# Stick-breaking attention summed by parts, with the value projection moved into half-size products

## The chip, the cores and the metric

The kernel runs on one core of a Trainium2 chip. The metric is the device time of one execution in microseconds (us), lower is better. Before the change three runs gave a median of 1948.08 us, from 1947.18 to 1949.51. The execution that was profiled took 1945.62 us.

## What is computed

One layer of a sequence model on a sequence of 1024 tokens with 1024 channels, all in float32. The part that the change touches is the mixer: a modulated RMS norm gives `h`, one projection of `h` gives q, k, v, three convolution inputs and two gates, and a stick-breaking attention with 16 heads of 64 channels runs on q, k, v:

```python
z = jnp.einsum('bhqd,bhkd->bhqk', qb, kp) * inv_sqrt          # strictly causal: s < t
log_not = jnp.where(mask, jax.nn.log_sigmoid(-z), 0.0)
excl = lax.cumsum(log_not, axis=3, reverse=True) - log_not
log_a = jax.nn.log_sigmoid(z) + excl
a = jnp.where(mask, jnp.exp(log_a), 0.0)
outs.append(jnp.einsum('bhqk,bhkd->bhqd', a, vp))
```

So the weight of key s for query t is sigmoid(z_ts) times the product of (1 - sigmoid(z_tj)) over the keys j between s and t. Then come a short gated convolution as a second branch, a projection of each branch, a merge by gates, an output projection, and a gated feed-forward network, each with a residual add.

## The kernel before, in words

**Number format.** Every matmul operand is split into a rounded part `hi` and a remainder `lo`, and a product is three matmuls: hi*hi, hi*lo, lo*hi. A split costs a ScalarE copy (`hi`) and a VectorE subtraction (`lo`).

**Half-size products.** Sections of the combined projection, and the feed-forward network, use a Strassen-Winograd scheme: a 1024x1024 product becomes seven products with 512 rows of weights and 512 tokens (`half_prod`, L117, twelve matmuls of 512 columns each). The weights' sums (`ws`, L587 to L590) are made on GpSimd. The factors of `h` are made once by `factors` (L342): it adds the two halves `hh` and `hl` of `h` back together (L348), makes the differences (L350 to L354), and splits the four results, which are called factor 5, 4, 6 and 3 (L356). Factors 5 and 4 stay in SBUF (`ft`); 6 and 3 go to DRAM (`d_t`) and are loaded back (L579, L581).

**Stages, in the order of time.**
1. Start, L142 to L330: modulation sums, the norm, and `h` made channel block by channel block (`make_h`, L260: two ScalarE passes and one GpSimd subtraction for each). TensorE already multiplies each finished block into the first seven of eight token blocks of the first 512 columns (`real`, L304). The order of the work here is pinned by `in_order`. The transposed input `xt` is kept in SBUF for this stage alone.
2. Projection by token blocks, the loop at L400: three chunks of 512 columns (the first half of v, then two halves of k), eight token blocks each, 24 matmuls of 512 columns for a block. A v block is split by `finish_v` (L391) and stored to `d_v`. A k block goes through `finish_k` (L369): square on ScalarE, sum on VectorE, reciprocal root on GpSimd (L113, L114), scaling on VectorE, four transposes on TensorE (L382), split, store to `d_k`. The steps of `factors` are spread over the k blocks.
3. Gates, the loop at L582: 20 sections of seven half-size products, first q (`put_q` after it), then the two convolution inputs (`put_u`), then the two gates. `later` drains the work that a section leaves over into the next products. Weight splits rotate through four buffers (`GS`), so ScalarE and VectorE run at most a few splits ahead of TensorE.
4. Attention: a generator `attention` (L756) emits 128 steps, one for a head h and a block i of 128 queries with n = 128(i+1) keys. `att_scores` (L691): two matmuls for each 512 keys into `z`; ScalarE takes a sigmoid of -z into `pt` (L705) and a sigmoid of z into `sg` (L706); VectorE runs a reversed running product over `pt` (the scan, L710) and multiplies `sg` by it, one place shifted (L712). One step later `att_trans` (L715) transposes `sg` on TensorE (L726) and splits it (L729, L730); for every second block, three steps later, `att_av` (L734) multiplies it by v (L741, L742), adds the two halves (L745, L746) and stores the head's rows of `d_ya` with a DMA on the SyncE queue (L748).
   Between these steps `fill` inserts pieces of `fillers` (L789) in proportion to the attention work done so far (`FILL`, `ATT`, `TAIL`): first the second half of v (L790 to L812, 384 matmuls of 256 columns), then the third convolution input (L814) and the second branch's projection (L840), 768 matmuls of 512 columns. `HEAD` pieces are put ahead of the first scores while the first head's q, k and v are loaded (L870 to L873).
5. The first branch's projection (L908 on), the output projection, the feed-forward network and its down projection.

A scheduler orders the instructions of each engine at build time; each engine then runs its own list strictly in that order and waits on semaphores. The DMAs that SyncE and ScalarE issue stand in those engines' lists too.

Of the kernel before, what the change touches and what calls it, by code (L numbers as in the profile page):

```python
# [8 lines left out]
F32 = mybir.dt.float32  # L9
# [7 lines left out]
P = 128  # L17
# [12 lines left out]
def block_kernel(tc, x, x_t, cols, ada_1, ada_2, ada_row, w_q, w_kv, w_v1, w_cg, w_a, w_b, w_o, w_g, w_u, w_d, out):  # L30
# [47 lines left out]
    d_t = {q: drp.tile([P, 2, 4, 512], F32, name=f"d_t{q}") for q in (6, 3)}  # L78
# [62 lines left out]
    sw = open_w("wpa", 3, 6)  # L141
# [17 lines left out]
    xt = sp.tile([P, KT, T], F32, name="xt")  # L159
# [13 lines left out]
    def load_wq(qt):  # L173
        wp, nraw, bufs = wps
        raw = wp.tile([P, 1024], F32, tag="raw", bufs=nraw, name=nm("raw"))
        nc.sync.dma_start(raw, w_kv[0, qt])
# [159 lines left out]
    ftx = ExitStack()  # L336
    ftp = ftx.enter_context(tc.tile_pool(name="phft", bufs=1, side="right", reuse_waits="tile"))
    ft = {q: ftp.tile([P, 2, 4, 512], F32R, name=f"ft{q}") for q in (5, 4)}
# [52 lines left out]
    def finish_v(ps, i, ch):  # L391
        vs = ap.tile([P, 8, P], F32R, tag="vs", bufs=3, name=nm("vs"))
        pv = ps.rearrange("p (h d) -> p h d", d=DH)
        nc.scalar.activation(vs[:, :, :DH], pv, AF.Copy)
        nc.vector.tensor_tensor(out=vs[:, :, DH:], in0=pv, in1=vs[:, :, :DH].bitcast(F32), op=ALU.subtract)
        nc.scalar.dma_start(d_v[8 * ch:8 * ch + 8, :, i, :].rearrange("h p d -> p h d"), vs.bitcast(F32))

    GR, NG, GS = 2, 2, 4
    tails = []
    for cc in range(3):  # L400
        w = wq if cc == 0 else [load_w(w_kv[cc, j]) for j in range(4)]
        for i in ((5, 6, 0, 1, 2, 3, 4, 7) if cc == 0 else range(8)):
# [15 lines left out]
            if (cc, i) == (2, 4):  # L418
# [32 lines left out]
    def w_of(sec, m):  # L451
        return w_q[m] if sec == 5 else w_cg[sec, m]
# [213 lines left out]
    for pt in pts:  # L666
        nc.gpsimd.memset(pt[:, D:D + 1], 0.0)
# [682 lines left out]
```

## Time and profile before

| | |
|---|---|
| median of 3 runs | 1948.08 us |
| the profiled execution, its own time | 1945.62 us |
| its span, first to last instruction | 1943.8 us |
| mean granted TensorE clock | 0.986 of full speed |
| TensorE busy (with matmul latency) | 1853.6 us, 95% |
| VectorE / ScalarE / GpSimd busy | 1462.3 / 864.6 / 673.7 us |
| stages by TensorE's own first and last instructions: start and token blocks to | about 204.6 us |
| gates to | 621.4 us |
| attention to | 1093.6 us |

How to read it: a matmul's row shows its latency, not what it costs when matmuls follow each other. A 512-column matmul shows some 0.39 us, but starts of neighbours stand 0.23 us apart. So TensorE's pace is read from how many matmuls fall into a stretch in which it never waits. "A <-B" behind a row names the engine and line whose end the instruction waited for.

### The profile page before, as it was taken

Reading aid. Unit: us, or ns where it says so; the run is one execution under the profiler, and the core shown is the slowest. Engines: PE = TensorE matmul, PEld = TensorE weight load, DVE = VectorE, ACT = ScalarE, POOL = GpSimd, SP = SyncE. Lnnn points to the kernel's source line nnn. Section 1 sums busy time; section 2 is a strip of 40 time slices with the busy share of each in tenths; the row PEclk is TensorE's granted clock in tenths of the full one; section 3 lists DMA queues with packets and bytes.
Section 4 is the critical chain, followed back from the end, with each engine's and each line's share of the span. In section 5 each row is a group of like instructions: output and inputs, shape, how many; then the busy total and the mean of one; then the engine's idle time right before and its main releaser. Section 6 shows DMA issues by size and latency. Waiting matters only on the chain.

```text
span 1943.8 us, 25154 instructions
## 1 busy us (share of the span) xinstructions
PE 1853.6 (95%) x8869; PEld 1519.5 (78%) x8869; DVE 1462.3 (75%) x1927; ACT 864.6 (44%) x1597; POOL 673.7 (35%) x475
## 2 busy tenths in 40 slices
PE   7899999998999999998999999979999999999899
PEld 4678767777888888887888788867888888878587
DVE  8865687778664799998999644499988788743854
ACT  4442343223333677776777421464444434422221
POOL 3694547978231001111000000065454444301713
PEclk8899999999999999999999999999999999999999
DMA  6465544334445756559554535323343334399566
GB/s 276 162 208 172 190 154 160 136 114 152 170 171 197 214 158 189 169 167 302 161 161 128 189 130 193 133 82 136 146 173 152 141 143 171 119 347 321 218 221 224
DMA packets 151149, 347.47 MB, mean 179 GB/s; under 512 B 15088, under 2 KB 52208, under 8 KB 149104
## 3 DMA queue, kind: packets, MB, share of 16 engines
q1 hardware_dynamic: 74000, 218.80, 34.4%
q10 hardware_dynamic: 76016, 123.40, 17.6%
q0 software_dynamic: 1008, 3.67, 0.5%
q8 instruction: 70, 1.15, 0.2%
q14 instruction: 55, 0.45, 0.1%
HBM read 235.19 MB, written 110.62 MB: 178 GB/s over the span
## 4 chain that ended last, share of the span: by engine, by line
PE 43%; DVE 10%; issue 3%; DMA 3%; ACT 2%; POOL 1%; ACTq 0%; SPq 0%; DVEq 0%; POOLq 0%
PE e L122 6%; PE e L124 6%; PE e L123 6%; PE e L1203 3%; PE e L1204 3%; PE e L1202 3%; PE pj L785 3%; PE pj L786 3%; PE pj L787 3%; DVE pt L710 2%; DVE wlo L965 2%; PE e L1020 1%; PE e L1022 1%; PE e L1021 1%; PE tr L726 1%
## 5 line engine op out<-in xcount | busy, mean ns | idle before, releaser
L710 DVE TENSOR_TENSOR_SCAN pt<-pt,dm 128x256 f32<-128x256 f32 (+7 forms) x128 | 173.9, 1363 | 5.3 <-ACT pt L705 5.1
L123 PE MATMUL e<-big,whi 128*128 128x512 f32 x352 | 138.0, 392 | 7.8 <-DVE big L127 7.8
L122 PE MATMUL e<-big,whi 128*128 128x512 f32 x352 | 137.7, 392 | 0.8 <-ACT c L1118 0.8
L124 PE MATMUL e<-big,wlo 128*128 128x512 f32 x352 | 137.5, 391 | 0.0
L1203 PE MATMUL e<-wlo,f 128*128 128x512 f32 (+1 forms) x319 | 123.1, 386 | 9.5 <-DVE wlo L965 9.5
L124 PE MATMUL pj<-big,wlo 128*128 128x512 f32 x320 | 127.0, 398 | 5.1 <-DVE wlo L127 5.1
L113 POOL TENSOR_SCALAR rs_m<-ss 128x1 f32<-128x1 f32 x8 | 2.0, 245 | 365.3 <-ACT xn L1035 365.3
L122 PE MATMUL pj<-big,whi 128*128 128x512 f32 x320 | 128.0, 400 | 0.4 <-ACT whi L438 0.4
L276 PE MATMUL pj<-whi,big 128*128 128x512 f32 x352 | 116.3, 410 | 11.6 <-ACT big L263 8.9
L123 PE MATMUL pj<-big,whi 128*128 128x512 f32 x320 | 127.1, 397 | 0.0
L705 ACT ACTIVATE pt<-z,rq 128x512 f32<-128x512 f32 (+2 forms) x192 | 112.3, 587 | 30.5 <-PE z L704 17.6
L1204 PE MATMUL e<-whi,f 128*128 128x512 f32 (+1 forms) x319 | 121.8, 382 | 0.0
L1202 PE MATMUL e<-whi,f 128*128 128x512 f32 (+1 forms) x319 | 118.5, 383 | 2.0 <-ACT fs L1142 1.4
L127 DVE TENSOR_TENSOR c<-e,c 128x512 f32<-128x512 f32 x154 | 102.8, 681 | 21.1 <-PE e L124 21.1
L829 POOL TENSOR_TENSOR ybl<-cy,ybh 128x512 fp32r<-128x512 f32 x16 | 29.0, 1810 | 255.7 <-ACT ybh L828 242.9
L438 ACT ACTIVATE whi<-raw 128x512 fp32r<-128x512 f32 x116 | 72.7, 633 | 94.4 <-PE pj L123 32.6
L706 ACT ACTIVATE sg<-z,rq 128x512 f32<-128x512 f32 (+1 forms) x192 | 112.7, 590 | 1.3 <-DVE mb L851 1.3
L127 DVE TENSOR_TENSOR c<-pj,c 128x512 f32<-128x512 f32 x140 | 93.2, 681 | 24.3 <-PE pj L124 24.1
L127 DVE TENSOR_TENSOR wlo<-ws,whi 128x512 fp32r<-128x512 f32 x80 | 73.6, 939 | 50.0 <-ACT whi L438 49.8
L730 DVE TENSOR_TENSOR atl<-tr,ath 128x512 fp32r<-128x512 f32 (+1 forms) x192 | 100.3, 544 | 10.7 <-ACT ath L729 10.3
L127 POOL TENSOR_TENSOR ws<-raw,raw 128x512 f32<-128x512 f32 x41 | 57.9, 1412 | 144.1 <-DMA raw<-w_cg 80.7
L729 ACT ACTIVATE ath<-tr 128x512 fp32r<-128x512 f32 (+1 forms) x192 | 90.4, 498 | 37.8 <-PE tr L726 12.7
(250 smaller groups left out, 5641.9 us busy)
## 6 DMA issues: line engine op xcount, KB each, us to landing
f<-d_f SPq DMA_DIRECT2D x77, 512.0 KB, 4.4
d_f<-fs ACTq DMA_DIRECT2D x70, 512.0 KB, 2.6
raw<-w_cg SPq DMA_DIRECT2D x40, 512.0 KB, 3.4
mada<-ada ACTq DMA_DIRECT2D x32, 512.0 KB, 4.2
raw<-w_g SPq DMA_DIRECT2D x24, 512.0 KB, 3.2
raw<-w_u SPq DMA_DIRECT2D x23, 512.0 KB, 3.2
d_k<-khl ACTq DMA_DIRECT2D x32, 256.0 KB, 2.2
d_q<-gt ACTq DMA_DIRECT2D x32, 256.0 KB, 2.1
```

Of the source, the lines that this page charges most:

```text
L122: nc.tensor.matmul(ps, wh[:, k, :], fh[:, k, :], start=(k == 0), stop=False)
L123: nc.tensor.matmul(ps, wh[:, k, :], fl[:, k, :], start=False, stop=False)
L124: nc.tensor.matmul(ps, wl[:, k, :], fh[:, k, :], start=False, stop=(k == 3))
L127: eng.tensor_tensor(out=out, in0=a, in1=b, op=op)
L276: nc.tensor.matmul(ps, a, b, start=(k == 0 and q == 0), stop=(k == KT - 1 and q == 2))
L705: nc.scalar.activation(pt[:, off + s0:off + s0 + m], z[:, :m], AF.Sigmoid, scale=rq[:, 1, i, h:h + 1])
L706: nc.scalar.activation(sg[:, s0:s0 + m], z[:, :m], AF.Sigmoid, scale=rq[:, 0, i, h:h + 1])
L710: nc.vector.tensor_tensor_scan(out=pt[:, rev], data0=pt[:, rev], data1=dm[:, rev], initial=0.0, op0=ALU.mult, op1=ALU.add)
L730: nc.vector.tensor_tensor(out=tl[:, :nb, c0:c0 + P], in0=src, in1=th[:, :nb, c0:c0 + P].bitcast(F32), op=ALU.subtract)
L1202: nc.tensor.matmul(o, sh, w[0][:, c], start=(j == 0), stop=False)
L1203: nc.tensor.matmul(o, sh, w[1][:, c], start=False, stop=False)
L1204: nc.tensor.matmul(o, sl, w[0][:, c], start=False, stop=(j == NJ - 1))
```

## The change

Four things are done together.

- **Attention summed by parts.** With R_s the running product over the keys from s on, the weight of key s is R_(s+1) - R_s. Moved onto the values this gives o_t = v_t + sum over s of R_s (v_(s-1) - v_s). So the scan's result `pt` is transposed itself; the second sigmoid (L706), the multiplication (L712) and the buffers `sg` go. The matrix that multiplies R is the difference of neighbouring values. The term v_t is written to `d_ya` ahead of time, and `att_av` adds onto it with an accumulating DMA, which is issued from GpSimd instead of SyncE.
- **Values by channel, in half-size products.** v becomes four more sections of the gates loop, at its head (24 sections instead of 20). A new `put_v` shifts, subtracts (GpSimd), stores v to `d_ya`, transposes the difference (TensorE), splits it through one buffer `vs` and stores it to `d_v`. The v chunk of the token blocks and the v fillers go, so the loop over token blocks has two chunks, both of k.
- **Factors in place.** `xt` is kept until the factors are made, and the differences are made in place in `xt`; the 16 additions of L348 go. Factor 4 joins 6 and 3 in DRAM (`d_t`) and is loaded back into the gates' pool. The pool of raw weights in the first stages has two buffers instead of three.
- **Planning numbers.** `FILL` goes from 2.5*16*5.2 to 2*16*5.2, and `HEAD` from 10 to 4 pieces.

```diff
     def factors():
         for j in range(4):
-            b = [[mp.tile([P, 512], F32, tag=f"tb{e}{n}", bufs=1, name=nm("tb")) for n in range(2)] for e in range(2)]
-            for e in range(2):
-                for n in range(2):
-                    tt(nc.gpsimd, b[e][n], hh[n][:, 4 * e + j, :].bitcast(F32), hl[n][:, 4 * e + j, :].bitcast(F32), ALU.add)
-                yield
+            b = [[xt[:, 4 * e + j, n * 512:(n + 1) * 512] for n in range(2)] for e in range(2)]
...
-    for cc in range(3):
-        w = wq if cc == 0 else [load_w(w_kv[cc, j]) for j in range(4)]
+    for cc in range(2):
+        w = wq if cc == 0 else [load_w(w_k[cc, j]) for j in range(4)]
...
-            if cc > 0:
-                tails.append(finish_k(ps, i, cc - 1))
-                next(tails[-1])
-            else:
-                finish_v(ps, i, 0)
-            for _ in range(2 if cc else 0):
+            tails.append(finish_k(ps, i, cc))
+            next(tails[-1])
+            for _ in range(2 if cc else 1):
                 next(ml, None)
...
-    gates = ([(5, j) for j in range(4)] + [(sec, j) for j in range(4) for sec in (1, 2)] +
+    gates = ([(sec, j) for sec in (6, 5) for j in range(4)] + [(sec, j) for j in range(4) for sec in (1, 2)] +
              [(sec, j) for sec in (4, 3) for j in range(4)])
...
+    def put_v(cf, m, n, left):
+        if n == 0:
+            nc.gpsimd.memset(cf[:, 1:2], 0.0)
+        else:
+            nc.gpsimd.tensor_copy(cf[:, 1:2], left[:, 513:514])
+        wt = g_tile()
+        tt(nc.gpsimd, wt, cf[:, 1:513], cf[:, 2:514], ALU.subtract)
+        nc.scalar.dma_start(d_ya[n][:, m, :], cf[:, 2:514])
+        yield
+        tr = ps_tr()
+        for i in range(4):
+            nc.tensor.transpose(tr[:, i * P:(i + 1) * P], wt[:, i * P:(i + 1) * P], ident)
+        vs = gp.tile([P, 2, 4, P], F32R, tag="vs", bufs=1, name=nm("vs"))
+        for h in range(2):
+            src = tr.rearrange("p (i d) -> p i d", d=P)[:, :, h * DH:(h + 1) * DH]
+            nc.scalar.activation(vs[:, h, :, :DH], src, AF.Copy)
+            tt(nc.vector, vs[:, h, :, DH:], src, vs[:, h, :, :DH].bitcast(F32), ALU.subtract)
+        nc.scalar.dma_start(d_v[2 * m:2 * m + 2, :, 4 * n:4 * n + 4, :].rearrange("h p i d -> p h i d"), vs.bitcast(F32))
...
         def later():
-            if pend:
+            if pendv:
+                next(pendv.pop(0), None)
+            elif pend:
                 put_q(*pend.pop(0))
-            elif g > 3:
+            elif g > 7:
...
             nc.scalar.activation(pt[:, off + s0:off + s0 + m], z[:, :m], AF.Sigmoid, scale=rq[:, 1, i, h:h + 1])
-            nc.scalar.activation(sg[:, s0:s0 + m], z[:, :m], AF.Sigmoid, scale=rq[:, 0, i, h:h + 1])
...
         nc.vector.tensor_tensor_scan(out=pt[:, rev], data0=pt[:, rev], data1=dm[:, rev], initial=0.0,
                                      op0=ALU.mult, op1=ALU.add)
-        nc.vector.tensor_tensor(out=sg[:, :n], in0=sg[:, :n], in1=pt[:, off + 1:D + 1], op=ALU.mult)
...
-                nc.tensor.transpose(tr[:, j * P:(j + 1) * P], sg[:, (b0 + j) * P:(b0 + j + 1) * P], ident)
+                nc.tensor.transpose(tr[:, j * P:(j + 1) * P], pt[:, off + (b0 + j) * P:off + (b0 + j + 1) * P], ident)
...
-        nc.sync.dma_start(d_ya[hf][e0:e0 + DH, pr, c0:c0 + 256], yv)
+        nc.gpsimd.dma_start(d_ya[hf][e0:e0 + DH, pr, c0:c0 + 256], yv, accum_op=ALU.add)
...
     def fillers():
-        for e in range(2):
-            w = []
...
-                nc.scalar.dma_start(d_v[8 + 4 * e:12 + 4 * e, :, i, :].rearrange("h p d -> p h d"), vs.bitcast(F32))
-                yield 1.3
         cb_w = {}
...
-    FILL = 2.5 * 16 * 5.2
+    FILL = 2 * 16 * 5.2
...
-    HEAD, TAIL = 10, 20.0
+    HEAD, TAIL = 4, 20.0
```

More of the change, by code (lines that the diff above doesn't have):

```diff
@@ L592, in block_kernel @@
             raws = two_raw(g + 1)
-        c11, c21, c12, c22 = (gp.tile([P, 512], F32, tag=f"c{q}", bufs=2, name=nm("c")) for q in range(4))
+        cfs = [gp.tile([P, 514], F32, tag=f"c{q}", bufs=2, name=nm("c")) for q in range(4)]
+        c11, c21, c12, c22 = (cf[:, 2:] for cf in cfs)
         def put(c, m, n):
-            if sec == 5:
+            if sec == 6:
+                if (m, n) == (j + 4, 1):
+                    return
+                f11, f21, f12, f22 = cfs
+                for a in (((f21, m, 0, None), (f22, m, 1, f21)) if m == j + 4 else ((f11, m, 0, None),) if n == 0 else
+                          ((f12, m, 1, f11),)):
+                    pv = put_v(*a)
+                    next(pv)
+                    pendv.append(pv)
+            elif sec == 5:
                 pend.append((c, m, n))
@@ L641, in block_kernel @@
                 pass
-        for _ in range((0 if sec == 5 else 3) if g + 1 < len(gates) else 50):
+        for _ in range((0 if sec >= 5 else 3) if g + 1 < len(gates) else 50):
             next(ml, None)
@@ L688, in block_kernel @@
     ats = {}
-    sgs = {}
+    ptof = {}
     def att_scores(h, i):
```

74 lines of the change are left out of this document (25 added, 49 removed).

## The prediction, made before the changed kernel was run

> **What bounds the kernel now.** I read the busy times by stage first, then the chain of waits, then each engine's costliest groups and TensorE's own waits inside the stages that change. Columns of the first view: stretch, then busy us (count) of TensorE, weight loads, VectorE, ScalarE, GpSimd, then clock and DMA.
>
> ```profile
> core 0: us, PE busy (x) PEld busy (x) DVE busy (x) ACT busy (x) POOL busy (x), PEclk, DMA share, GB/s
> 85.00:204.00 119.00, 116.91 (x543) 95.51 (x542) 67.72 (x84) 40.99 (x66) 84.09 (x69) 1.00 0.61 200
> 204.00:621.00 417.00, 402.51 (x1715) 316.26 (x1714) 305.37 (x365) 143.18 (x238) 240.18 (x156) 0.99 0.43 153
> 621.00:1094.00 473.00, 449.64 (x2757) 391.45 (x2756) 431.11 (x619) 341.60 (x732) 29.14 (x20) 0.99 0.63 186
> 1094.00:1184.00 90.00, 90.00 (x387) 72.29 (x386) 42.33 (x64) 19.44 (x32) 0.00 (x0) 1.00 0.42 142
> ```
> ```profile
> PE 43%; DVE 10%; issue 3%; DMA 3%; ACT 2%; POOL 1%; ACTq 0%; SPq 0%; DVEq 0%; POOLq 0%
> ```
>
> TensorE carries the chain in every stage. In the gates (204 to 621) VectorE has slack, in attention (621 to 1094) it is busy 431.1 of 473 us, so there TensorE and VectorE are both nearly full. Everything from 1094 on is untouched and I carry it over.
>
> TensorE's price per matmul: 90.00 us over 387 back-to-back matmuls of 512 columns is 0.2326 us. The next views give the token blocks' pace, a group of four transposes, and the value fillers.
>
> ```profile
> 111.13 0.39 PE L276 MATMUL pj<-whi,big 128*128 128x512 f32 x1
> ...
> 113.40 0.60 PE L382 MATMUL tr<-dm,qn 128*128 128x128 f32 x4
> 113.75 0.48 PE L276 MATMUL pj<-wlo,big 128*128 128x512 f32 x1
> 114.07 0.63 PE L276 MATMUL pj<-whi,big 128*128 128x512 f32 x2
> ```
> ```profile
> 621.50:632.50 11.00, 11.00 (x94) 10.99 (x93) 3.63 (x7) 2.97 (x7) 0.19 (x4) 1.00 1.01 285
> ```
>
> Ten matmuls start between 111.13 and 113.40: 0.227 us each. Four transposes take 0.35 us and slow the next matmul by 0.09: 0.0875 to 0.11 us each. A 256-column matmul takes 11.00/94 = 0.117 us.
>
> **The change part by part. TensorE's own work.** The value chunk of the token blocks goes: 8 x 24 = 192 matmuls x 0.227 = -43.6 us. The value fillers go: 384 x 0.117 = -44.9. Four gate sections come: 4 x 84 = 336 x 0.2326 = +78.2. Their 64 transposes: x 0.11 = +7.0. Net -3.3: the half-size products save little, because they bring transposes. So waits decide.
>
> **Waits before the gates.** The token blocks lose the value chunk, which needed no norm. Now the seven blocks begun in the start stage all end together and each needs the k norm:
>
> ```profile
> L371 ACT ACTIVATE qsq<-pj 128x512 f32<-128x512 f32 x16 | 9.5, 594 | 39.5 <-PE pj L276 28.7 <-DVE vs L395 3.4 <-DVE qn L376 2.6
> L373 DVE TENSOR_REDUCE qss<-qsq 128x8 f32<-128x512 f32 x16 | 10.9, 681 | 14.5 <-ACT qsq L371 14.5
> L376 DVE TENSOR_TENSOR qn<-pj,rs_r 128x512 f32<-128x512 f32 x16 | 11.0, 690 | 15.9 <-POOL rs_r L114 15.9
> ```
> ```profile
> L114 POOL TENSOR_TENSOR rs_r<-rs_m,nhalf 128x8 f32<-128x8 f32 x16 | 27.5, 1716 | 0.8
> L113 POOL TENSOR_SCALAR rs_m<-qss 128x8 f32<-128x8 f32 x16 | 4.3, 271 | 28.8 <-DVE qss L373 28.2
> ```
>
> In the changed program's TensorE list the transposes of three blocks stand in front of the second k chunk's first matmul. The third is ready after 0.6 + 0.7 + 3 x 2.0 (GpSimd, one at a time) + 0.7 = 8 us and some semaphore time, with about 1 us of matmuls to cover it. I take 8 us of idle TensorE (from 4, if the first blocks end earlier, to 14, if VectorE's factor splits push in between). All of the second chunk is queued behind. A long wait also costs clock:
>
> ```profile
> 206.86 0.57 PE L122 MATMUL pj<-ft,whi 128*128 128x512 f32 x1 [2.06 <-ACT whi L438]
> ...
> 208.94 0.63 PE L122 MATMUL pj<-ft,whi 128*128 128x512 f32 x1
> 209.36 0.63 PE L123 MATMUL pj<-ft,whi 128*128 128x512 f32 x1
> ...
> 210.62 0.39 PE L123 MATMUL pj<-ft,whi 128*128 128x512 f32 x1
> 210.84 0.39 PE L124 MATMUL pj<-ft,wlo 128*128 128x512 f32 x1
> ```
>
> Behind this 2.06 us wait eight matmuls start 0.43 us apart instead of 0.23: 1.6 us more. So +9.6 us. The wait quoted here, at the first gate, should go, since GpSimd has nothing ahead of the weight sums by then: -3.7 (at worst 0). *A rule beside it:* the Trainium skill, "TensorE: Matmul & The Clock Gate", section "What's actually happening", has the clock at half rate only after an idle window of about 3.4 us, for about 3.4 us. The length agrees with these rows, the threshold does not, as 2.06 us were enough; by the rule the last term would be -2.1 and the sum -8.8.
>
> The in-place differences move into the start stage's GpSimd list, between the subtractions that make `hl`; nine of them, 1.5 us each, fit in its idle time but may delay `hl`: +1 (0 to 5). The 16 additions that go (1.49 us each) stood beside matmuls: 0. Two raw buffers instead of three, and factor 4's trip through DRAM (2 MB more to load while the first two sections' 48 matmuls run): 0, up to 5 if that load is late.
>
> **The four value sections.** Per section TensorE needs 84 x 0.2326 + 16 x 0.11 = 21.3 us. Each has four `put_v`, and they share one buffer `vs`, so ScalarE's copy waits until the previous store has landed.
>
> ```profile
> L809 ACT ACTIVATE vs<-pj 128x256 fp32r<-128x256 f32 x16 | 6.3, 393 | 17.5 <-DMA d_v<-vs 11.4 <-PE pj L806 4.0 <-PE tr L726 2.0
> ```
> ```profile
> d_v<-vs ACTq DMA_DIRECT2D x8, 512.0 KB, 4.4
> d_t<-ts ACTq DMA_DIRECT2D x8, 512.0 KB, 3.4
> sqt<-d_q SPq DMA_DIRECT2D x32, 256.0 KB, 5.4
> d_f<-fs POOLq DMA_DIRECT2D x7, 512.0 KB, 7.4
> d_ya<-oy SPq DMA_DIRECT2D x64, 64.0 KB, 2.6
> ```
>
> The row shows that ScalarE already waits for such stores. A turn of the buffer is two copies (0.39 each), two VectorE halves (0.41 each, L810 below), 0.4 to issue, and the landing. The new store has 2 KB rows like `d_t<-ts` (3.4 us): 5.4 us a turn, 86 us for 16 turns against TensorE's 85. With the 4.4 us of `d_v<-vs` it is 6.4 x 16 = 102. While ScalarE waits, the weight splits behind it wait, and then TensorE. I take the landing near `d_t`: +5 (0 to 17).
>
> **Attention.**
>
> ```profile
> L710 DVE TENSOR_TENSOR_SCAN pt<-pt,dm 128x256 f32<-128x256 f32 (+7 forms) x128 | 173.9, 1363 | 5.3 <-ACT pt L705 5.1
> L730 DVE TENSOR_TENSOR atl<-tr,ath 128x512 fp32r<-128x512 f32 (+1 forms) x192 | 100.3, 544 | 10.7 <-ACT ath L729 10.3
> L712 DVE TENSOR_TENSOR sg<-sg,pt 128x128 f32<-128x128 f32 (+7 forms) x128 | 99.5, 783 | 5.7 <-ACT sg L706 0.6 <-DVE pt L710 0.5 <-ACT pt L705 0.5
> L810 DVE TENSOR_TENSOR vs<-pj,vs 128x256 fp32r<-128x256 f32 x16 | 6.6, 413 | 13.8 <-ACT vs L809 13.8
> ```
> ```profile
> L706 ACT ACTIVATE sg<-z,rq 128x512 f32<-128x512 f32 (+1 forms) x192 | 112.7, 590 | 1.3 <-DVE mb L851 1.3
> ```
> ```profile
> PE o L741 <- ACT ath L729: 8.9, 4, 4.4
> PE tr L726 <- DVE atl L730: 6.9, 13, 1.5
> ```
>
> VectorE loses L712 and L810, 106 us, and falls to about 325 busy; ScalarE loses 112.7 of 341.6. TensorE now: fillers 768 x 0.2326 = 178.6, values 44.9, scores 147,456 columns at 0.2326 per 512 = 67, L741/L742 512 x 0.117 + 128 narrow ones x 0.0875 = 71, transposes 576 x 0.0875 to 0.11 = 50 to 63; in all 412 to 425 of the 472 us from 621.4 to 1093.6. So 47 to 60 us are waits and stretched starts. With VectorE at 325 of some 405 us I let half of them go: -25 (0 to -50). What is late next is the scan itself, then ScalarE's `ath`.
>
> The start of attention gets worse: before, ten value pieces covered the load of head 0.
>
> ```profile
> 618.83 0.53 SPq L677 DMA_DIRECT2D sqt<-d_q  x1
> ...
> 627.63 0.54 SPq L680 DMA_DIRECT2D vt<-d_v  x1
> ```
>
> These loads spread over 9 us of SyncE's list and land 5.4 us later; four pieces of 6 matmuls cover 5.6 us. Three loads of weights stand ahead in the new list, the third waiting for a split. I take 4.4 us of wait and 1.6 of slow clock: +6 (0 to 11), all scores queued behind. `d_ya` moves from SyncE to GpSimd's list, where only 16 subtractions (29.1 us busy) stand; even landing in 7.4 instead of 2.6 us, the last store is not needed until some 10 us after attention's last product: 0, up to 5.
>
> **Sum.** -3.3 + 9.6 - 3.7 + 1 + 5 - 25 + 6 = -10.4 us. The profiled execution took 1945.6 us (span 1943.8), so 1935.2; it lies 2.5 under the median of 1948.1, which gives **1937.7 us**.
>
> **The rivals.**
> - *Attention is set free wholly.* All 50 us of stalls go and the first loads are covered: 25 + 6 less, 1906.7. For: VectorE at 91% explains most of it. Against: a TensorE in strict order never runs without waits.
> - *Slower: attention keeps its waits.* TensorE waits for a chain, sigmoid, scan, transpose, copy, and not for VectorE's load. The quoted waits end on `ath` (8.9) and `atl` (6.9), neither of which the change touches. Then the -25 is 0: 1962.7. It decides when fewer than 15 us go.
> - *The one buffer paces the value sections.* At a landing of 4.4 us +17 instead of +5: 1949.7; beyond that each further us costs 16.
> - *The change frees nothing because the DMA that adds is slow* and the first branch's projection waits: over 10 us a store; little speaks for it.
>
> **How the numbers follow.** Forecast (1923 to 1944) 0.45, wholly free 0.15, attention keeps its waits 0.22, the buffer 0.16, the last 0.02. A measurement tells about 0.2%, 4 us, from no change. Faster: 0.45 + 0.15, less a little for the forecast's edge, 0.58. The buffer's case lies half within 0.2%: same 0.12. Slower 0.30. The range runs from the wholly free case to the one that keeps its waits, 1906 to 1964.
>
> **What would show it.** Right: a TensorE wait of about 8 us on `qn` near 95 us; value sections of about 22.5 us each; gates ending near 670 instead of 621; attention about 408 long, VectorE near 325 in it; nothing changed behind. Wrong: an attention over 430 us whose transposes wait as before; `whi` splits waiting for `d_v<-vs` in every value section; TensorE waiting on `yr`.

## The result, and the profile after

The changed kernel takes 1956.89 us (median of 9 runs, 1951.95 to 1960.62); the kernel before, run beside it, 1947.18. The ratio is 1.006, with a 95% interval of 1.0043 to 1.0078: 0.6% **slower**, where 0.5% faster was forecast. The profiled execution took 1956.52 us, its span is 1954.7 (before: 1943.8), its granted clock 0.975 (0.986).

The first view is the stages: stretch, then busy us (count) of TensorE, weight loads, VectorE, ScalarE and GpSimd, then clock and DMA. First the start stage of the kernel before, then all stages of the changed one.

```profile
0.00:81.00 81.00, 59.83 (x214) 41.71 (x215) 70.48 (x121) 38.96 (x61) 34.66 (x31) 0.87 0.61 234
```
```profile
0.00:88.00 88.00, 65.95 (x213) 46.67 (x214) 76.45 (x121) 39.73 (x63) 45.42 (x39) 0.79 0.53 204
88.00:166.00 78.00, 66.24 (x304) 54.33 (x304) 50.27 (x65) 31.24 (x52) 46.42 (x41) 0.91 0.66 215
166.00:684.00 518.00, 501.75 (x2174) 397.91 (x2171) 360.68 (x460) 175.95 (x305) 293.97 (x210) 0.98 0.46 166
684.00:1105.00 421.00, 400.19 (x2367) 345.39 (x2368) 334.45 (x465) 248.12 (x515) 77.92 (x80) 0.98 0.71 195
1105.00:1195.00 90.00, 90.00 (x388) 72.36 (x387) 42.72 (x64) 20.42 (x33) 0.00 (x0) 1.00 0.39 135
```

```profile
L731 DVE TENSOR_TENSOR_SCAN pt<-pt,dm 128x256 f32<-128x256 f32 (+7 forms) x128 | 176.8, 1387 | 47.8 <-ACT pt L727 47.6
```

In attention VectorE fell from 431 to 334 us, as forecast, and it is no longer full: the row of the scan now has 47.8 us of idle time ahead of it, where it had 5.3. The last stage is the same. Two things are new: a start stage that is 7 us longer, with eight more GpSimd instructions in it and a lower clock, and token blocks in which TensorE is busy for only 66 of 78 us.

The next table cuts every kernel of this study at the same four places of TensorE's own timeline: the start of the last product of the modulation sums (`acc`), of the first gate product, of the last gate product, and of the last filler product. In us:

| kernel | start | token blocks | gates | attention | rest | span |
|---|---|---|---|---|---|---|
| before | 80.0 | 112.5 | 428.7 | 471.7 | 851.0 | 1943.8 |
| **changed** | 87.4 | 79.0 | 516.9 | 421.3 | 850.0 | 1954.7 |
| x1 factors after the start | 78.4 | 91.1 | 521.3 | 423.6 | 850.6 | 1965.0 |
| x2 factors after the norms | 79.1 | 76.8 | 523.5 | 423.1 | 851.5 | 1954.0 |
| x3 loads later | 87.4 | 79.4 | 530.5 | 417.9 | 850.5 | 1965.7 |
| x4 raw weights' place | 86.8 | 80.6 | 514.7 | 415.9 | 849.9 | 1947.9 |
| x5 two sigmoids | 87.4 | 79.5 | 517.9 | 457.1 | 851.7 | 1993.6 |
| x6 before, attention alone | 80.4 | 112.5 | 427.0 | 448.4 | 852.3 | 1920.6 |
| x7 plain store | 87.9 | 78.6 | 522.7 | 433.1 | 852.4 | 1974.8 |
| x8 combined | 79.0 | 76.0 | 522.5 | 414.4 | 852.3 | 1944.2 |
| x9 first branch held | 87.1 | 80.7 | 518.6 | 414.7 | 851.0 | 1952.1 |
| x10 first gate on VectorE | 87.9 | 78.6 | 520.8 | 422.5 | 850.9 | 1960.8 |
| x11 combined 2 | 79.1 | 78.6 | 517.0 | 406.9 | 853.1 | 1934.7 |
| x12 combined 3 | 79.1 | 78.7 | 527.4 | 405.4 | 852.2 | 1942.8 |

Each row is one execution. Where neither a stage nor anything ahead of it was edited, the gates read 514.7 to 522.7 (changed, x4, x5, x7, x9), and attention, where it was not edited, 417.9 to 423.6 (changed, x1, x2, x3, x10). So a difference of less than some 8 us in the gates, or 6 us in attention, is read only together with the wait that explains it.

Against the forecast's steps, changed minus before: start +7.4 (forecast +1), token blocks -33.5 (-34.0), gates +88.2 (+86.5), attention -50.4 (-63.9), rest -1.0 (0). These are the rows behind the four places that differ, first TensorE's waits in the order of time:

```profile
84.21 1.22 PE L281 MATMUL pj<-whi,big 128*128 128x512 f32 x2 [5.39 <-ACT big L268]
...
111.55 1.08 PE L380 MATMUL tr<-dm,qn 128*128 128x128 f32 x4 [9.69 <-DVE qn L374]
114.54 0.87 PE L380 MATMUL tr<-dm,qn 128*128 128x128 f32 x3 [1.90 <-DVE qn L374]
...
185.67 0.80 PE L122 MATMUL pj<-ft,whi 128*128 128x512 f32 x1 [6.94 <-ACT whi L427]
...
688.86 0.79 PE L804 MATMUL pj<-big,whi 128*128 128x512 f32 x1 [5.10 <-ACT whi L427]
...
699.82 0.77 PE L725 MATMUL z<-skh,sqt 128*128 128x128 f32 x2 [3.42 <-DMA skh<-d_k]
```

*The start stage.* VectorE and GpSimd in the timeline around 78 us:

```profile
77.07 1.77 DVE L127 TENSOR_TENSOR ft<-xt,ft 128x512 fp32r<-128x512 f32 x1
78.77 1.48 DVE L209 SCALAR_TENSOR_TENSOR acc<-ada,ca,acc 128x256 f32<-128x256 f32 x1
...
80.77 0.47 DVE L209 SCALAR_TENSOR_TENSOR acc<-ada,ca,acc 128x256 f32<-128x256 f32 x1
```
```profile
78.25 1.71 POOL L127 TENSOR_TENSOR xt<-xt 128x512 f32<-128x512 f32 x1
```

The same instruction takes 0.47 us while GpSimd has nothing to do, and 1.48 us beside its difference. VectorE sets the pace of the start stage (it is busy for 70.5 of 81 us before), so what GpSimd does in "idle time" is paid by VectorE, and two splits of factors (`ft`) have been put into its list as well. The forecast counted only GpSimd's time.

*The first gate.* ScalarE's timeline ahead of the wait at 185.67; ACTq rows are the time that ScalarE spends on issuing DMAs:

```profile
173.45 5.29 ACTq L386 DMA_DIRECT2D d_k<-khl  x2
178.87 0.69 ACT L383 ACTIVATE khl<-tr,cst 128x512 fp32r<-128x512 f32 x1 [5.44 <-PE pj L124]
179.58 4.38 ACTq L386 DMA_DIRECT2D d_k<-khl  x2
184.01 1.08 ACT L640 ACTIVATE c<-pj 128x512 f32<-128x512 f32 x2 [4.46 <-issue]
184.98 1.15 ACT L427 ACTIVATE whi<-ws 128x512 fp32r<-128x512 f32 x2
```

Four stores of k hold ScalarE for 9.7 us (elsewhere such a store is mostly issued in 0.37 us), while SyncE's queue moves 6 MB of factors. The copy and the splits that TensorE needs stand behind them.

*Attention.* Two loads on SyncE's queue, and two rows of ScalarE:

```profile
672.39 0.80 SPq L673 DMA_DIRECT2D big<-d_h  x2
683.79 0.81 SPq L419 DMA_DIRECT2D raw<-w_cg  x2
```
```profile
755.88 0.63 ACT L914 ACTIVATE ya<-yr 128x512 fp32r<-128x512 f32 x1 [5.21 <-DMA yr<-d_ya]
...
805.88 0.63 ACT L914 ACTIVATE ya<-yr 128x512 fp32r<-128x512 f32 x1 [3.35 <-DMA yr<-d_ya]
```

The first fillers' weights can't be loaded before the last gate product has run (10 us behind the loads ahead of them). And two splits of the *next* stage's input stand in the middle of attention in ScalarE's list, where they wait for the load of what attention has only just stored.

### The profile page after: what moved, and what is told of

Its sections match the earlier page's. It is cut to its first block, busy times and chain, and to the rows that moved or that the text cites. A ratio compares the mean times of both kernels' runs of the same rounds, so it can differ in the third digit from the quotient of the medians.

```text
span 1954.7 us, 24786 instructions
## 1 busy us (share of the span) xinstructions
PE 1856.4 (95%) x8693; PEld 1517.7 (78%) x8693; DVE 1410.8 (72%) x1851; ACT 793.2 (41%) x1433; POOL 746.2 (38%) x567
## 4 chain that ended last, share of the span: by engine, by line
PE 71%; DVE 11%; DMA 6%; POOL 5%; issue 4%; ACT 2%; ACTq 1%; SPq 0%; DVEq 0%; POOLq 0%
PE e L122 6%; PE e L123 6%; PE e L124 6%; PE pj L122 5%; PE pj L124 5%; PE pj L123 5%; PE pj L804 4%; PE pj L805 4%; PE pj L806 4%; PE e L1199 3%; PE e L1200 3%; PE e L1198 3%; PE tr L746 3%; PE pj L281 2%; DVE acc L209 2%
## 5 line engine op out<-in xcount | busy, mean ns | idle before, releaser
L731 DVE TENSOR_TENSOR_SCAN pt<-pt,dm 128x256 f32<-128x256 f32 (+7 forms) x128 | 176.8, 1387 | 47.8 <-ACT pt L727 47.6
L124 PE MATMUL pj<-big,wlo 128*128 128x512 f32 x384 | 153.1, 400 | 5.0 <-DVE wlo L127 5.0
L122 PE MATMUL pj<-big,whi 128*128 128x512 f32 x384 | 153.4, 400 | 0.2 <-ACT whi L427 0.2
L123 PE MATMUL pj<-big,whi 128*128 128x512 f32 x384 | 152.9, 398 | 0.0
L768 POOL DMA_DIRECT2D d_ya<-oy x64 | 52.8, 825 | 262.1 <-DVE oy L766 225.2
L127 DVE TENSOR_TENSOR c<-pj,c 128x512 f32<-128x512 f32 x168 | 112.2, 684 | 34.9 <-PE pj L124 34.6
L127 DVE TENSOR_TENSOR wlo<-ws,whi 128x512 fp32r<-128x512 f32 x96 | 87.8, 930 | 59.5 <-ACT whi L427 58.6
L122 PE MATMUL pj<-ft,whi 128*128 128x512 f32 x288 | 116.5, 405 | 8.9 <-ACT whi L427 8.9
L127 POOL TENSOR_TENSOR ws<-raw,raw 128x512 f32<-128x512 f32 x45 | 63.1, 1403 | 154.8 <-DMA raw<-w_cg 100.7
L127 DVE TENSOR_TENSOR c<-e,c 128x512 f32<-128x512 f32 x154 | 102.9, 682 | 20.6 <-PE e L124 20.6
L123 PE MATMUL pj<-ft,whi 128*128 128x512 f32 x288 | 115.1, 400 | 0.0
L124 PE MATMUL pj<-ft,wlo 128*128 128x512 f32 x288 | 114.5, 401 | 0.6 <-DVE wlo L127 0.6
L804 PE MATMUL pj<-big,whi 128*128 128x512 f32 x256 | 105.8, 413 | 6.5 <-ACT whi L427 5.1
L127 POOL TENSOR_TENSOR ws<-raw,ws 128x512 f32<-128x512 f32 x66 | 102.7, 1556 | 22.4 <-DVE wlo L961 20.7
```

The lines of the kernel that those rows point to most:

```text
L122: nc.tensor.matmul(ps, wh[:, k, :], fh[:, k, :], start=(k == 0), stop=False)
L123: nc.tensor.matmul(ps, wh[:, k, :], fl[:, k, :], start=False, stop=False)
L124: nc.tensor.matmul(ps, wl[:, k, :], fh[:, k, :], start=False, stop=(k == 3))
L127: eng.tensor_tensor(out=out, in0=a, in1=b, op=op)
L731: nc.vector.tensor_tensor_scan(out=pt[:, rev], data0=pt[:, rev], data1=dm[:, rev], initial=0.0, op0=ALU.mult, op1=ALU.add)
L804: nc.tensor.matmul(ps, wh, rh_, start=(k == 0), stop=False)
```

## The experiments

Kernels are named as in the table. Ratios are to the kernel before, run beside each of them; each comes with its 95% interval.

**x1: the differences behind the start stage.** All four lines of a step are queued behind `lasthl`, GpSimd's last subtraction that makes `hl`:

```diff
-            tt(nc.gpsimd, b[0][1], b[0][1], b[0][0], ALU.subtract)
+            with tc.issue_after(lasthl[0].ins):
+                tt(nc.gpsimd, b[0][1], b[0][1], b[0][0], ALU.subtract)
```

> The changed kernel, with all 16 of GpSimd's in-place differences queued behind the last subtraction that makes hl. In the changed kernel nine of them stand between those subtractions, VectorE's products beside them take 1.38 to 1.75 us instead of 0.48 to 0.68, and the start stage's last product is at 87.8 us instead of 80.4, behind a wait of 5.4 us on ScalarE's copy into hh. Theory (the differences cost the start stage its 7 us): VectorE's products take 0.48 us again to the stage's end, the 5.4 us wait goes, the last product is at 80 to 81 us. The whole gains 7 us if the k-norm chain behind it is left as it is, 0 to 3 us if the differences then stand in that chain's way (its wait of 11.8 us becomes longer by what the start stage gained). Rival (the start stage is late for another reason, such as two raw weight buffers instead of three): its last product stays near 87 us.

Measured: 1.0077 (1.0047 to 1.0108). The start stage ends at 78.4 us, the token blocks take 12 us more, and the wait for the norms is now

```profile
113.35 1.09 PE L384 MATMUL tr<-dm,qn 128*128 128x128 f32 x4 [21.00 <-DVE qn L378]
```

It follows that the differences, with the two splits that they let into VectorE's list, cost the start stage its 7 us, and more. VectorE's multiply-adds in the start stage, before, changed and x1:

```profile
L204 DVE SCALAR_TENSOR_TENSOR acc<-ada,ca,acc 128x256 f32<-128x256 f32 x42 | 33.0, 786 | 0.9
```
```profile
L209 DVE SCALAR_TENSOR_TENSOR acc<-ada,ca,acc 128x256 f32<-128x256 f32 x42 | 36.6, 870 | 0.8
```
```profile
L209 DVE SCALAR_TENSOR_TENSOR acc<-ada,ca,acc 128x256 f32<-128x256 f32 x42 | 31.1, 740 | 0.9
```

The changed kernel has 3.6 us more of them than the kernel before, 1.0 us more of other products (on `xt`), and 2.6 us of `ft` splits, 7.2 us in all; so about a third of the loss is work that came earlier, and the rest is instructions that became longer. Moved back, the differences stand ahead of the reciprocal roots in GpSimd's list, and all of the gain is lost there.

**x2: the factors behind the first chunk's norms.** The same edit, with the last reciprocal root of the first chunk in place of `lasthl`, and all steps of `factors` spread over the second chunk.

> The changed kernel, with the whole making of the factors (GpSimd's differences, and with them ScalarE's copies, VectorE's subtractions and the stores) begun only after the first k chunk's norms. Theory (the early factors cost both the start stage and the k-norm chain): start stage's last product at 80 to 81 us instead of 87.8; the wait of TensorE on qn behind the first chunk falls from 11.8 to the 8 us that the prediction worked out from the chain alone, as ScalarE's squares and VectorE's sums no longer stand behind copies and splits of factors; the first gate product comes 9 to 11 us earlier (near 156 us) and the whole gains that, 1945 to 1948. Rival 1 (the chain is as long without them): only the 7 us of the start stage go. Rival 2 (the factors are now late): TensorE waits for them or for the gates' weights near 140 to 160 us, and the gain is lost there.

Measured: 1.0033 (1.0011 to 1.0054), an interval that overlaps the changed kernel's, so the gain in total is not certain. The first gate product comes 10.5 us earlier (155.9), in the theory's range. TensorE's waits for the norms:

```profile
98.20 0.63 PE L385 MATMUL tr<-dm,qn 128*128 128x128 f32 x4 [2.04 <-DVE qn L379]
99.69 0.63 PE L385 MATMUL tr<-dm,qn 128*128 128x128 f32 x4 [0.86 <-DVE qn L379]
```

With one of 0.2 us ahead of them they come to 3.1 us, not the 8 that were expected: the chain alone costs less, and in the changed kernel GpSimd's differences and the copies and splits of factors stood between its steps. Rival 2 has a share, though. The factors now end late, waits of 2.3 us (on a norm, at 132) and 3.5 us (on the gates' first weights, at 155.9) follow, and the token blocks as a whole are only 2.2 us shorter. The gates read 6.6 us longer, 0.8 us above the highest of the unedited ones.

**x3: the loads of factors 6 and 3 later.**

```diff
-    for q in (4, 6):
-        nc.sync.dma_start(ft[q].bitcast(F32), d_t[q])
+    nc.sync.dma_start(ft[4].bitcast(F32), d_t[4])
...
+        if g == 0:
+            ra = g_raw(w_of(*gates[1]))
+            with tc.issue_after(last_raw[0].ins):
+                nc.sync.dma_start(ft[6].bitcast(F32), d_t[6])
+                for e in range(2):
+                    nc.sync.dma_start(fac[3][e].bitcast(F32), d_t[3][:, e])
```

> The changed kernel, with the loads of factor 6 and factor 3 (4 of the 6 MB that are loaded around the first gate) queued on SyncE behind the first weights of the second gate. In the changed kernel TensorE waits 6.9 us at the first gate's third product for a split of ScalarE, which was issuing stores of k that took 4.5, 1.3 and 3.1 us instead of 0.37 each, while these loads ran. Theory (the loads fill the DMA queues, a store's issue then holds ScalarE, and the split behind it is late): the stores' issues take about 0.4 us, the wait falls to 2 us or less, the gate stage becomes 5 us shorter unless product 7 or 4 then waits for its late factor (up to 3 us). Rival (GpSimd's weight sums are what is late): the wait stays at 6 to 7 us.

Measured: 1.0106 (1.0086 to 1.0127), slower still, and yet the theory's first half holds. The first pair of stores of k (the second takes 1.19 us), and the first product with factor 5, which follows without a wait:

```profile
173.87 1.15 ACTq L386 DMA_DIRECT2D d_k<-khl  x2
```
```profile
179.06 0.50 PE L122 MATMUL pj<-ft,whi 128*128 128x512 f32 x1
```

Four stores take 2.3 us instead of 9.7 (5.29 and 4.38). But the second gate's other weights now stand behind these loads, and with them GpSimd's list: TensorE waits 10.5 us for a difference of values at 195.6.

**x4: another place for the raw weights.**

```diff
     gw = gws.enter_context(tc.tile_pool(name="wpb", bufs=1, side="right", reuse_waits="tile"))
+    for tag in ("whi", "wlo"):
+        gw.tile([P, 512], F32R, tag=tag, bufs=GS, name=nm("first"))
```

> The changed kernel, with the attention stage's weight pool laid out in another order: the split weights first, the raw weights behind them. In the changed kernel the first two loads of raw weights wait 9.9 us on SyncE for the last product of the gates, and attention starts with waits of 5.1 us (on the split of these weights) and 3.8 us (on the first head's keys, loaded behind them). Theory (the smaller factor pool moved the raw buffers onto the place of the gates' split weights, which the last product still reads): the loads are issued near 675 instead of 683.8 us, both waits go or fall below 2 us in all, and the time falls by 6 to 9 us. Rival (too few filler pieces ahead of the first scores, whatever the place): the first wait goes but the one on the keys stays or grows, and 0 to 5 us are gained.

Measured: 1.0061 (1.004 to 1.0082), no different from the changed kernel in time. In the profile the loads start at 674.2, and the waits are

```profile
685.07 0.50 PE L806 MATMUL pj<-big,whi 128*128 128x512 f32 x1 [2.54 <-ACT whi L427]
...
696.23 0.77 PE L727 MATMUL z<-skh,sqt 128*128 128x128 f32 x2 [5.03 <-DMA skh<-d_k]
```

The place explains the first wait (5.1 to 2.5). The second one grew, as the rival said: the head's loads still stand behind a third load of weights, and four filler pieces don't cover them. The table has attention 5.4 us shorter, but TensorE's waits in it fall only from 20.6 to 19.8 us.

**x5: the second sigmoid and the multiplication put back; x6: the kernel before, with attention's part alone.** x5 adds to the changed kernel, and x6 takes from the kernel before, these lines and the buffer `sg` (in x5 `sg` also takes the places of two tiles `yx` in the list for the next stage's input):

```diff
-            nc.scalar.activation(sg[:, s0:s0 + m], z[:, :m], AF.Sigmoid, scale=rq[:, 0, i, h:h + 1])
-        nc.vector.tensor_tensor(out=sg[:, :n], in0=sg[:, :n], in1=pt[:, off + 1:D + 1], op=ALU.mult)
```

> The changed kernel, with attention's second sigmoid and the multiplication by the shifted scan put back (112.7 us of ScalarE, 99.5 of VectorE); values stay differences, so what is computed isn't the reference. Theory (VectorE's load made half of attention's waits): in the kernel before, TensorE's attention stage held 31 us of waits and 27 us of stretched starts over its floor of 414 us; in the changed kernel 20 us of waits, 4.4 of them at the stage's start, and 28 of stretched starts over 369. So attention becomes 13 to 17 us longer (421 to 434 to 438), all of it in waits on atl and ath. The prediction's size: 25 us longer. Rival (TensorE waits for the chain of sigmoid, scan, transpose and copy, not for VectorE's load): within 5 us of 421.

> The kernel before, with attention's part of the change alone: one sigmoid, the scan, and the transposes read the running products; values, fillers, gates and the store stay as they were, so what is computed isn't the reference. Theory: attention 13 to 17 us shorter (472 to 455 to 459), nothing else moves, 1928 to 1932 against a profiled 1945.6. The prediction's size: 25 us shorter, 1921. Rival (attention keeps its waits): within 5 us of before.

Measured: x5 1.0255 (1.0238 to 1.0272), attention 35.8 us longer; x6 0.9898 (0.9883 to 0.9913), attention 23.3 us shorter and nothing else moved. TensorE's waits in attention (engine, line, what it waited for: us, times, longest), behind the first scores; x6, then x5:

```profile
PE tr L721 <- DVE atl L725: 4.5, 5, 1.3
PE z L700 <- ACT pt L702: 2.5, 3, 1.3
...
```
```profile
PE tr L751 <- DVE atl L755: 13.8, 17, 1.4
PE tr L751 <- DVE sg L737: 8.3, 11, 1.4
PE o L766 <- DVE oy L771: 4.2, 5, 2.0
...
```

My theory's 13 to 17 us was too small, the prediction's 25 was close, and the rival that attention keeps its waits is refuted. The two operations are worth 23 us where the value fillers stand between the steps, and 36 where they don't. TensorE's waits in the whole stage are 22.6 us before and 9.9 in x6, 20.6 in the changed kernel and 40.4 in x5, so they make 13 of the 23 us and 20 of the 36. That the fillers had covered some of VectorE's lateness is the likely reason for the difference; no run shows it by itself. One more thing follows from the table: in x5 the value fillers have gone and the two operations stand, and attention is only 14.6 us shorter than before, though 44.9 us of TensorE's work have left it.

**x7: attention's result stored by SyncE, without adding.**

```diff
-        nc.gpsimd.dma_start(d_ya[hf][e0:e0 + DH, pr, c0:c0 + 256], yv, accum_op=ALU.add)
+        nc.sync.dma_start(d_ya[hf][e0:e0 + DH, pr, c0:c0 + 256], yv)
```

> The changed kernel, with attention's result stored by SyncE as before, without adding to what stands in DRAM; the part that the values' own columns contribute is lost, so what is computed isn't the reference. Theory (the adding store is off the path): attention and all behind it within 3 us of the changed kernel. Rival (its 64 issues of 0.83 us on GpSimd slow VectorE's scan, or the first branch waits for its landing): attention or what lies behind it becomes over 5 us shorter, and the scan's mean falls from 1387 towards 1363 ns.

Measured: 1.0141 (1.0124 to 1.0158), attention 11.8 us *longer*; neither was expected. The scan's mean stays (1386 ns) and so does the rest (852.4 us), so neither of the rival's two harms shows. On SyncE a store stands in line with the heads' loads and waits for its sum (83.0 us in all); a load of keys behind such stores came late:

```profile
932.41 1.27 ACT L727 ACTIVATE pt<-z,rq 128x512 f32<-128x512 f32 x2 [9.42 <-DMA skl<-d_k]
```

**x8: combined.** x2's edit from the third norm on, x4's, and the following (`ld0` is the last load of head 0):

```diff
-        vs = gp.tile([P, 2, 4, P], F32R, tag="vs", bufs=1, name=nm("vs"))
         for h in range(2):
+            vs = g_tile(F32R).rearrange("p (i d) -> p i d", d=P)
...
-                cb_w[m] = load_ch(w_cg[0, m])
+                with tc.issue_after(ld0[0].ins) if m > 1 else ExitStack():
+                    cb_w[m] = load_ch(w_cg[0, m])
...
-    HEAD, TAIL = 4, 20.0
+    HEAD, TAIL = 8, 20.0
```

> The changed kernel with what the first four runs point to: the making of the factors queued behind the third norm of the first k chunk (behind the last it ended so late that the gates' first weights came late), the value store's tile taken from a ring of four half-size tiles, the raw weights of attention laid out as in the run before, the third filler's weights loaded behind the first head, and eight filler pieces instead of four ahead of the first scores. Theory: start stage's last product at 79 us, first gate product near 153, gate stage 512 to 517, attention 411 to 415 (both waits at its start gone), the rest 850: 1926 to 1935 in all, under the kernel before. Rival 1 (factors that start earlier slow the norms again): first gate product at 158 to 166, 1935 to 1945. Rival 2 (attention's start has another wait behind these): attention stays at 416 or more.

Measured: 1.0022 (1.0005 to 1.0039). Start 79.0, first gate product 154.9 and attention 414.4 are as expected. The gates are not:

```profile
168.20 9.37 ACTq L391 DMA_DIRECT2D d_k<-khl  x2
177.62 1.09 ACT L647 ACTIVATE c<-pj 128x512 f32<-128x512 f32 x2 [9.45 <-issue]
```
```profile
179.27 0.80 PE L124 MATMUL pj<-ft,whi 128*128 128x512 f32 x1 [11.67 <-ACT whi L434]
```

What the earlier stages gain, one pair of stores takes back: everything ahead of the gates is earlier, but the loads are as many, and ScalarE is held for 9.4 us.

**x9: the first branch held back; x10: the first gate's copy and splits on VectorE.** In x9 `late` holds head 13's last `otmp` and `oy`, and the last load issued by then, behind which the loads of `yr` stand; in x10 `g_split` makes `hi` with `nc.vector.tensor_copy` where its second argument is true, for `s1` and `s3` too, and the first copy into `c11` is VectorE's:

```diff
+            with tc.issue_after(late[0].ins), tc.issue_after(late[1].ins):
                 nc.scalar.activation(h_, yr, AF.Copy)
                 tt(nc.vector, l_, yr, h_.bitcast(F32), ALU.subtract)
```
```diff
-        p6 = g_prod(g_split(s2_), 5)
+        p6 = g_prod(g_split(s2_, g == 0), 5)
```

> The changed kernel, with the loads and splits of the first branch's input (yr and ya) queued behind the last outputs of head 13. In the changed kernel two of them, for which two spare tiles had become free, stand in the middle of attention in ScalarE's list: at 755.9 and 805.9 us ScalarE is idle for 5.2 and 3.4 us until the load of what attention just stored has landed, and TensorE's waits on pt of 1.8 and 0.6 us follow. Theory (a part of attention's lost gain is these two): both waits go, attention 417 to 420 instead of 421.3, the total 1 to 5 us less. Rival (they hide behind TensorE's fillers): attention within 1 us, or the splits that now come later make the end of attention longer.

> The changed kernel, with the first gate's first copy out of PSUM and its three splits of weight sums made by VectorE instead of ScalarE; loads and stores as they were. Theory (ScalarE's list stands still at stores of k whose issue takes 4.5 and 3.1 us while 6 MB of factors load): TensorE's wait of 6.9 us for the first weight sum's split goes or falls below 2 us though nothing about the data has changed, and the gate stage becomes 4 to 7 us shorter, unless factor 4's load then comes late (up to 3 us). Rival (the sums on GpSimd are late): the wait stays at 6 to 7.

Measured: x9 1.005 (1.0028 to 1.0073), x10 1.006 (1.0041 to 1.008). In total time neither can be told from the changed kernel. In the profile x9's attention is 6.6 us shorter, and the waits on `pt` fall; the changed kernel's, then x9's:

```profile
PE z L725 <- ACT pt L727: 4.6, 5, 1.8
PE tr L746 <- DVE atl L750: 4.1, 6, 1.0
...
```
```profile
PE tr L747 <- DVE atl L751: 4.0, 4, 1.9
...
PE z L726 <- ACT pt L728: 1.3, 2, 1.0
```

TensorE's waits in the whole stage fall from 20.6 to 17.1 us, so the rows account for 3.5 of the 6.6. x11 below has the same edit and x8 hasn't: there the waits on `pt` are 1.2 us against 8.6, and attention 406.9 against 414.4.

In x10 the stores hold ScalarE as before (6.0 and 2.7 us), and TensorE waits 3.4 us instead of 6.9:

```profile
173.57 5.99 ACTq L386 DMA_DIRECT2D d_k<-khl  x2
```
```profile
182.26 0.47 PE L122 MATMUL pj<-ft,whi 128*128 128x512 f32 x1 [3.41 <-DVE whi L428]
```

The wait of 6.9 us is the highest of its kind: in x4, x5, x7 and x9, which have nothing edited ahead of it, it is 4.7, 4.7, 5.9 and 4.8. So VectorE's splits save 1.3 to 3.5 us. What is left goes back to the same stores, for VectorE's list has a last block of k ahead of these splits, and that waits for ScalarE:

```profile
180.41 0.75 DVE L384 SCALAR_TENSOR_TENSOR khl<-tr,cst,khl 128x512 fp32r<-128x512 f32 x1 [6.08 <-ACT khl L383]
```

ScalarE's `khl` starts at 179.69, behind the pair of stores at 173.57. The gate stage as a whole shows no gain (520.8, inside the spread).

**x11: x8 with x9's and x10's edits; x12: x11 with the halves of factors 4 and 6 in other places** (`f4h` where raw weights were, `f4l` where the first chunk's weights were).

```diff
-    for q in (4, 6):
-        ft[q] = gp.tile([P, 2, 4, 512], F32R, name=f"ft{q}")
+    f4h = half("4h")
+    gp.tile([P, D], F32, tag="mada", bufs=2, name=nm("first"))
+    f4l = half("4l")
```

> The combined kernel of before, in which TensorE waited 11.7 us at the first gate because a store of k took 8.6 us to issue on ScalarE, with the first gate's copy and splits on VectorE and the first branch's loads and splits held behind head 13. Theory: the wait falls to 4 us or less (factor 4 lands near 175), gate stage 512 to 516, attention 408 to 412: 1930 to 1936 profiled, 0.4 to 0.8% under the kernel before. Rival (the loads are late in any case): wait on factor 4 of 8 us or more, 1938 to 1942.

> The kernel of the run before this one, with the halves of factors 4 and 6 laid out so that three of the four stand where weights were that are done with early: their loads needn't wait for the last token block. Theory: they are issued near 156 instead of 165 us, no wait on a factor is left at the first gate, 1926 to 1933 profiled. Rival (the queues are full either way, and the k stores then land later): no gain over the run before.

Measured: **x11 0.9972 (0.9955 to 0.999)**, 1936.97 us: faster than the kernel before and than the changed one. The theory's range for the profiled execution, 1930 to 1936, is missed by 0.5 us. TensorE's wait at the first gate is 2.98 us although two stores hold ScalarE for 9.0 us, where x8 had 11.67 us behind a hold of 9.4; beside x3 this is the clearest sign that the wait came from ScalarE's list. Attention takes 406.9. x12 1.0021 (1.0 to 1.0041): the factors' loads are issued no earlier (from 167.3 us), and the new layout put a gate's tile where the k blocks had been, so that GpSimd waited for a store of k to land, and TensorE for 15.6 us at the first gate:

```profile
184.18 0.24 POOL L584 MEMSET c<- 128x1 f32 x3 [14.21 <-DMA d_k<-khl]
```

## Why the prediction was wrong

**What held.** TensorE's own work: the token blocks, gates and fillers cost what they were counted at. The four value sections run without a wait of TensorE between 191 and 285 us, so the rival of the single buffer falls: its +5 was 0, though ScalarE waited 21.8 us for the buffer's stores to land. Attention's -25 was near the mark for the two operations in the kernel before (x6: -23.3), and the rival that attention keeps its waits was wrong. Nothing changed behind.

**Right by luck.** The value chunk with the norms was put at -43.6 + 9.6, and -33.5 was measured. But the forecast took its 8 us from the chain of the norms alone, and in x2 that chain makes TensorE wait for 3.1. The changed kernel waits for 9.7 + 1.9 = 11.6, because the making of the factors stands between the chain's steps, which the forecast had only as its upper case.

**The steps that failed**, with what the forecast put and what was measured:

1. *"nine of them, 1.5 us each, fit in its idle time but may delay `hl`: +1 (0 to 5)."* It was +7.4. The differences went where the forecast said, but they lengthened VectorE's instructions (one from 0.47 to 1.48 us, 4.6 us in all) and let 2.6 us of splits into its list, and VectorE paces that stage. x1 and x2 show it: without them the stage ends at 78.4 and 79.1. The Trainium skill, "SBUF — State Buffer", section "SBUF: two separate sides", says that a GpSimd instruction that reads SBUF and a VectorE instruction with two SBUF inputs exclude each other for their whole length. The rows above agree roughly: VectorE's instruction of 1.48 us starts inside GpSimd's of 1.71 and ends at 80.25, 0.3 us behind its end at 79.96. A reader of that page would have asked, for each step given to an idle GpSimd, what VectorE does beside it.
2. *"The wait quoted here, at the first gate, should go, since GpSimd has nothing ahead of the weight sums by then: -3.7 (at worst 0)."* The wait grew from 2.1 to 6.9 us, so the term was +4.9 instead of -3.7 (at least +2.6, by the 4.7 us of x4 and x5). The row named ScalarE's split, and the forecast blamed the engine that feeds it. The kernel before already shows another cause: GpSimd is done with its sums at 200.8 us, and ScalarE is held by two stores of k until 205.2.

```profile
199.50 1.29 POOL L590 TENSOR_TENSOR ws<-raw,ws 128x512 f32<-128x512 f32 x1
```
```profile
201.83 3.33 ACTq L388 DMA_DIRECT2D d_k<-khl  x2
205.21 1.08 ACT L617 ACTIVATE c<-pj 128x512 f32<-128x512 f32 x2 [3.41 <-issue]
```

The change left these stores where they were, and a pair of them now takes 4.4 to 5.3 us to issue while 6 MB are loaded (x3, x10, and x11 against x8 show that the wait comes from there). "Factor 4's trip through DRAM: 0, up to 5 if that load is late" looked at the load's landing, not at what else uses the queues meanwhile. That it is this trip's 2 MB which lengthened the hold is likely, but no run takes them alone away.
3. *Attention's sum.* -44.9 - 25 + 6 took the rest of attention's list as it was. The change also put two new tiles, `yx`, first in the list of places for the next stage's input (a line not in the diff above), and so that stage's first splits could start in the middle of attention (x9: 6.6 us, of which waits explain 3.5). In x6 the same two tiles stand eighth and ninth in that list, and no split comes before 1020 us. At the start TensorE waits for 8.9 us, where the forecast had 4.4 and 1.6 of slow clock, because the weights' raw buffers came to lie on tiles that the last gate product still reads (x4: the first wait 5.1 to 2.5) and four filler pieces don't cover the head's loads behind a third load of weights (x8, with eight pieces and that load later, has no such wait). With both mended, and eight filler pieces ahead, x11's attention is 406.9 us, where the forecast's terms give 471.7 - 63.9 = 407.8. That they meet within 1 us is partly luck, for of the forecast's +6 at the start only a wait of 2.5 us is left there. The single effects of 5 to 7 us are each little more than the spread of one execution; the 14 us together are well outside it. TensorE's waits fall by 9.3 of these 14 us (20.6 to 11.3); the rest isn't traced to a row.

Added up, changed minus before against the forecast: start 6.4 too little counted, token blocks 0.5, gates 1.7 (the first gate 8.6 in this execution, less 5 for the buffer; the 1.9 that are then left over are inside the stage's spread), attention 13.5, rest -1.0. That is 21.1 us, the distance from -10.4 to the measured +10.7 of the table.

x11 shows the other side: with the list positions and places mended, the profiled execution takes 1936.47 us, and the sum on record for it was 1935.2. By stage it stands at -0.9, -33.9, +88.3, -64.8 and +2.1 against the kernel before, where the forecast had +1, -34.0, +86.5, -63.9 and 0. x11 has edits that nobody forecast, so this is no proof; but it fits the reading that the operations were priced about rightly, and that the forecast took for granted where the scheduler and the pools would put them.

What stays open: whether the gates of x2 are longer at all, and the part of attention's 14 us that no wait shows. How far the 36 us of x5 come from missing cover alone was not separated from its other waits.

## What to carry to other kernels

Count a step that moves to an "idle" engine at what it does to the engine that shares its memory access, and to the list of every engine that it feeds; the place in the list matters as much as the price. When a change frees or moves a tile, ask which waiting load or later stage will now use that place. In these runs an engine that issues stores stood still while large loads were under way, so the work that the bounding engine waits for is better given there to another engine, if that one doesn't itself wait for the first (x10).

## What the runs showed of the hardware

- A store of 256 KB in rows of 512 B is mostly issued on ScalarE in 0.37 us. While 6 MB of factors were loaded, two of them took 5.3 us, and 9.4 us in x8 (where 397 GB/s were moved from 156 to 178 us), and the engine did nothing else meanwhile.
- VectorE's 128x256 multiply-add of two SBUF inputs took 0.47 us, and 1.48 beside a GpSimd subtraction of 128x512; its 128x512 subtraction went from 0.68 to 1.77 us.
- A DMA that adds to DRAM costs GpSimd 0.83 us to issue (64 of them, 52.8 us), and it doesn't lengthen VectorE's scan: 1387 ns on average with it, 1386 without (x7).
